# The first layer's beginning: half-tile loads, a fixed order of scaling and splitting, and more warming matmuls

## The chip, the cores and the metric

The kernel runs on one core of a Trainium2 chip. The metric is device time in microseconds of one execution, as the median of three runs. The engines are TensorE (PE, with its weight loads as PEld), VectorE (DVE), ScalarE (ACT), GpSimd (POOL) and SyncE (SP); SP issues nearly all DMAs here.

## What is computed

Two pre-norm decoder layers on 256 tokens of 1024 channels in float32. Each layer normalises, multiplies by one wide input projection, runs three groups of heads side by side, projects back, and then runs a squared-ReLU MLP:

```python
for l in range(DEPTH):                       # DEPTH = 2, x is (1, 256, 1024)
    h = rms_norm(x, ln1_gain[l])
    proj = h @ w_in[l]                       # 1024 x 2866, cut into 15 parts
    ...                                      # sparse attention, latent attention, retention
    x = x + mixed @ w_out[l]
    h = rms_norm(x, ln2_gain[l])
    x = x + jnp.square(jax.nn.relu(h @ w_up[l])) @ w_down[l]
return rms_norm(x, final_gain)
```

with `rms_norm(x, g) = x * rsqrt(mean(x*x) + eps) * g`. Only the beginning of layer 0 is touched by the change.

## The kernel before

**Products.** A float32 product is made of three float32r matmuls (`mm3`, L144 to L148): each operand is split into a high part, cast by ACT (L140), and a low part, source minus high part, by DVE (L141). x stands as 2 tiles t of 128 tokens, with 1024 channels in two halves h of 512; `xT` holds it transposed and split, 8 blocks of 128 channels, and is the stationary operand. The factor `rstd` of the norm is not in `xT`: it is applied when the accumulated result is taken out of PSUM by ACT (`scaled`, L570). The channel gain is in `xT`.

**The input projection** goes by chunks of columns in the order A, B2, B1, B3, rq, rk, rg, rv (`inproj`, L555). A chunk is loaded in units of 2 or 3 channel blocks; chunk A has 434 columns and four units of 2 blocks (434 KB each), so 48 matmuls: 12 per unit. Chunk A fills two accumulator banks, one per t, of the only two that the tag `acc` has; chunk B2 needs them next.

**The weight stream** (`Stream`, L265) hands out, in a fixed list, loads and splits of units. A raw unit lives in one of 5 raw buffers until it is split, its high and low part in one of 5 split buffers until its matmuls are done. Loads are issued by SP in order. Behind chunk A the list has small vectors, `uq` and `uk` (weights of the latent attention), B2, two sets of small tables (`w2s`, and `pos_t` in 16 DMAs of 8 KB, L404), `c1` (1056 KB of constants), B1, the four `w1` units (2 MB, L415), which are used straight from their raw buffers and not split, and B3.

**Order.** The framework orders each engine's instructions ahead of time, by priority and by the times that it reckons. `prio(key)` lifts a block by so many places (`split`: 800). `tc.issue_after(ins)` puts a block's instructions that are on the engine of `ins` behind it in that engine's queue.

**The beginning of layer 0.** SP issues c0 (identity and rope frequencies), half (0,0) of x, the gain g8, half (0,1), weight unit A0, all of tile 1 of x, then A1, A2, A3 (L167 to L179, L323). PE runs 8 warming matmuls of 128x128 (L176), then for each (t, h) in `norm_half` (L487) four transposes (L493); DVE multiplies 512 columns by the gain (L500), ACT casts them (L140), DVE subtracts (L141). Units A1 and A2 have their low part made by POOL (`START_POOL`). The sums of squares (`sum_sq`, L510, ACT) come behind the last half's cast, then `mean_sq` (DVE) and the power on POOL (L194) give `rstd`. The rope tables (L200) are some 30 small DVE instructions and two Sin on ACT (L228, L229); nothing ties their place.

Of the kernel before, what the change touches and what calls it, by code (L numbers as in the profile page):

```python
# [14 lines left out]
P = 128  # L15
# [28 lines left out]
    'pol': -100, 'norm': 100, 'act': 200, 'split': 800,  # L44
}

PIECES = {'A': 2, 'B1': 4, 'B2': 2, 'B3': 4, 'rk': 2, 'rg': 4, 'rv': 2, 'wo': 2, 'wu': 2}

START_POOL = (1, 2)

MAGIC = 12582912.0
PI_LO = 3.1415925
# [25 lines left out]
def tile_hybrid_trunk(  # L78
# [65 lines left out]
    def mm3(o, a, b, start, stop):  # L144

        nc.tensor.matmul(o, a[1], b[0], start=start, stop=False)  # L146
        nc.tensor.matmul(o, a[0], b[1], start=False, stop=False)  # L147
        nc.tensor.matmul(o, a[0], b[0], start=False, stop=stop)  # L148

    def bcast_row(t, row, n):  # L150
        nc.sync.dma_start(t, row.unsqueeze(0).broadcast_to([P, n]))
# [22 lines left out]
    ps_idle = acc("ps_idle")  # L174
    for _ in range(WARM):
        nc.tensor.matmul(ps_idle[:, 0:P], idle, idle, start=True, stop=True)  # L176
# [139 lines left out]
    def add_unit(key, pieces, n, eng=nc.vector):  # L316

        name = "_".join(str(z) for z in key)

        def load():  # L320
            raw = raw_tile(name)
            for view, src in pieces:
                nc.sync.dma_start(view(raw), src)  # L323
            return raw

        def split_(raw):
            p = hilo(name)
            m = n // PIECES.get('A0' if key[:2] == (0, 'A') else key[1], 1)
            for o in range(0, n, m):
                split(p[0][:, o:o + m], p[1][:, o:o + m], raw[:, o:o + m], eng)  # L330
            return p

        W.add(key, load, split_)
# [150 lines left out]
    xT2 = p1.tile([P, 8, 2, S], F32R, name="xT", tag="xT")  # L484
    xT = [xT2[:, :, i] for i in range(2)]

    def norm_half(t, h, gain, eng=nc.vector):  # L487
        sl = slice(h * 512, (h + 1) * 512)
        xg = scr("xg", [P, 512])
        ps = wk("ps_xT", "MN"[h])  # L490
        if gain is None:
            for j in range(4):
                nc.tensor.transpose(ps[:, j * P:(j + 1) * P], xs[:, t, h * 512 + j * P:h * 512 + (j + 1) * P], ident)  # L493
            if t == h == 0:

                ps_g = acc("ps_g")
                nc.tensor.transpose(ps_g[:, 0:8], g8, ident[0:8, 0:8])
                nc.vector.tensor_copy(gT, ps_g[:, 0:8])
            xg = xg.rearrange("p (k c) -> p k c", k=4)
            nc.vector.tensor_tensor(xg, ps.rearrange("p (k c) -> p k c", k=4),  # L500
                                    gT[:, 4 * h:4 * h + 4].unsqueeze(2).broadcast_to([P, 4, P]), op=ALU.mult)
            dst = (slice(None), slice(4 * h, 4 * h + 4), slice(t * P, (t + 1) * P))
            return split(xT[0][dst], xT[1][dst], xg)
# [24 lines left out]
    for l in range(DEPTH):  # L528
# [5 lines left out]
        rstd = p2.tile([P, 2], F32, name=L + "rstd", tag="rstd")  # L534
        hrstd = p2.tile([P, 2], F32, name=L + "hrstd", tag="hrstd")
        if l == 0:
            for t in range(2):
                for h in range(2):
                    last = norm_half(t, h, None)
            with tc.issue_after(last[0].ins):  # L540
                for t in range(2):
                    for h in range(2):
                        sum_sq(t, h, ss1)
        else:
            ss1 = ss_next
        for t in range(2):
            mean_sq(ms1, ss1, t)
            rsqrt(rstd[:, t:t + 1], ms1[:, t:t + 1])
            nc.gpsimd.tensor_scalar(hrstd[:, t:t + 1], rstd[:, t:t + 1], 0.5, None, op0=ALU.mult)

        if l == 0:
            rope_tables()
# [624 lines left out]
```

## Time and profile before

| | us |
|---|---|
| median of 3 runs (lowest, highest) | 675.86 (675.41, 676.44) |
| the profiled execution, its own time | 675.34 |
| its span, first to last instruction | 673.5 |
| PE busy in the span | 651.4 (97%) |
| DVE / ACT / POOL busy | 452.4 / 379.3 / 68.0 |

Times inside the trace count from the span's start. The profiled execution has 1.84 us around its span, and is 0.52 us below the median. A busy PE is a PE with an instruction in flight, at whichever clock; so a stretch with the lower granted clock counts as busy too.

### The profile page before, as it was taken

Reading aid. Unit: us, or ns where it says so; the run is one execution under the profiler, and the core shown is the slowest. Engines: PE = TensorE matmul, PEld = TensorE weight load, DVE = VectorE, ACT = ScalarE, POOL = GpSimd, SP = SyncE. Lnnn points to the kernel's source line nnn. Section 1 sums busy time; section 2 is a strip of 40 time slices with the busy share of each in tenths; the row PEclk is TensorE's granted clock in tenths of the full one; section 3 lists DMA queues with packets and bytes.
Section 4 is the critical chain, followed back from the end, with each engine's and each line's share of the span. In section 5 each row is a group of like instructions: output and inputs, shape, how many; then the busy total and the mean of one; then the engine's idle time right before and its main releaser. Section 6 shows DMA issues by size and latency. Waiting matters only on the chain.

```text
span 673.5 us, 10414 instructions
## 1 busy us (share of the span) xinstructions
PE 651.4 (97%) x3639; PEld 551.9 (82%) x3639; DVE 452.4 (67%) x1051; ACT 379.3 (56%) x887; POOL 68.0 (10%) x116
## 2 busy tenths in 40 slices
PE   7988999999999999999999999999999999999995
PEld 6987978676788888888889998876688888888884
DVE  6755967677756666666685597677686666666664
ACT  5857776364645454545466786637284454545442
POOL 3510401201000000000023132111100000000000
PEclk7999999999999999999999999999999999999999
DMA  7898544122865656565648574331275656565511
GB/s 232 261 186 257 168 126 123 44 94 68 269 204 165 218 169 215 167 215 167 175 139 200 168 240 133 93 95 34 92 254 181 220 169 208 172 203 181 195 62 62
DMA packets 79508, 111.58 MB, mean 166 GB/s; under 512 B 9432, under 2 KB 67680, under 8 KB 79328
## 3 DMA queue, kind: packets, MB, share of 16 engines
q1 hardware_dynamic: 79424, 110.92, 53.9%
q8 instruction: 28, 0.46, 0.3%
q14 instruction: 24, 0.20, 0.1%
q0 software_dynamic: 32, 0.00, 0.0%
HBM read 109.86 MB, written 1.05 MB: 165 GB/s over the span
## 4 chain that ended last, share of the span: by engine, by line
PE 87%; DMA 5%; DVE 4%; ACT 1%; issue 1%; SPq 1%; POOL 0%; POOLq 0%; ACTq 0%; DVEq 0%
PE ps_up L1023 17%; PE l_pd L146 9%; PE l_pd L147 9%; PE l_pd L148 8%; PE ps_up L1024 8%; PE l_po L146 2%; PE l_po L148 2%; PE l_po L147 2%; PE l_oT L856 2%; DMA raw_B<-in_w_in_dram 2%; PE l_B L146 1%; PE l_B L147 1%; PE l_B L148 1%; PE ps_pT L864 1%; PE ps_s L146 1%; DMA raw_wu<-in_w_up_dram 1%
## 5 line engine op out<-in xcount | busy, mean ns | idle before, releaser
L1023 PE MATMUL ps_up<-xT,hi_wu 128*128 128x512 f32 x512 | 180.0, 394 | 1.3 <-DVE u_s L1035 1.3
L1024 PE MATMUL ps_up<-xT,lo_wu 128*128 128x256 f32 x512 | 140.7, 279 | 0.0
L1023 PEld LDWEIGHTS ps_up<-xT,hi_wu 128*128 128x128 f32 x512 | 95.7, 187 | 24.0 <-DVE u_s L1035 1.7
L141 DVE TENSOR_TENSOR lo_wd<-raw_wd,hi_wd 128x1024 fp32r<-128x1024 f32 x64 | 78.2, 1225 | 52.5 <-ACT hi_wd L140 52.2
L147 PE MATMUL l_pd<-lo_wd,u_h 128*128 128x512 f32 x256 | 100.1, 391 | 0.0
L146 PE MATMUL l_pd<-hi_wd,u_l 128*128 128x512 f32 x256 | 100.1, 391 | 0.0
L148 PE MATMUL l_pd<-hi_wd,u_h 128*128 128x512 f32 x256 | 99.6, 389 | 0.0
L1024 PEld LDWEIGHTS ps_up<-xT,lo_wu 128*128 128x128 f32 x512 | 96.0, 188 | 1.7
L140 ACT CAST hi_wu<-raw_wu 128x512 fp32r<-128x512 f32 x128 | 72.5, 617 | 38.9 <-issue 28.1
L141 DVE TENSOR_TENSOR lo_wu<-raw_wu,hi_wu 128x512 fp32r<-128x512 f32 x128 | 82.2, 687 | 16.6 <-ACT hi_wu L140 16.4
L140 ACT CAST hi_wd<-raw_wd 128x1024 fp32r<-128x1024 f32 x64 | 67.0, 1049 | 32.1 <-PE l_pd L148 21.4
L146 PEld LDWEIGHTS l_pd<-hi_wd,u_l 128*128 128x128 f32 x256 | 48.0, 188 | 10.8
L148 PEld LDWEIGHTS l_pd<-hi_wd,u_h 128*128 128x128 f32 x256 | 48.1, 188 | 10.4
L147 PEld LDWEIGHTS l_pd<-lo_wd,u_h 128*128 128x128 f32 x256 | 48.1, 188 | 8.9
L140 ACT CAST u_h<-u_u 128x512 fp32r<-128x512 f32 x32 | 19.8, 620 | 55.4 <-DVE u_u L1037 55.4
L141 DVE TENSOR_TENSOR lo_B<-raw_B,hi_B 128x192 fp32r<-128x192 f32 (+1 forms) x80 | 28.7, 415 | 23.9 <-ACT hi_B L140 23.8
L1034 ACT COPY u_s<-ps_up 128x256 f32<-128x256 f32 x64 | 23.3, 368 | 36.1 <-PE ps_up L1024 36.1
L1035 DVE TENSOR_TENSOR u_s<-ps_up,u_s 128x256 f32<-128x256 f32 x64 | 26.7, 421 | 24.8 <-ACT u_s L1034 24.8
L140 ACT CAST hi_B<-raw_B 128x192 fp32r<-128x192 f32 (+1 forms) x80 | 25.1, 381 | 18.6 <-DMA raw_B<-in_w_in_dram 13.7
L146 PE MATMUL l_B<-hi_B,xT 128*128 128x384 f32 x96 | 32.9, 351 | 2.3 <-ACT q_sb L570 2.3
L141 DVE TENSOR_TENSOR u_l<-u_u,u_h 128x512 fp32r<-128x512 f32 x32 | 22.1, 691 | 17.8 <-ACT u_h L140 17.8
L148 PE MATMUL l_B<-hi_B,xT 128*128 128x384 f32 x96 | 32.4, 338 | 0.0
(321 smaller groups left out, 1246.5 us busy)
## 6 DMA issues: line engine op xcount, KB each, us to landing
raw_wu<-in_w_up_dram SPq DMA_DIRECT2D x64, 512.0 KB, 4.6
raw_wd<-in_w_down_dram SPq DMA_DIRECT2D x64, 512.0 KB, 4.2
raw_B<-in_w_in_dram SPq DMA_DIRECT2D x24, 384.0 KB, 3.6
raw_wo<-in_w_out_dram SPq DMA_DIRECT2D x10, 512.0 KB, 3.6
raw_A<-in_w_in_dram SPq DMA_DIRECT2D x8, 434.0 KB, 5.0
raw_wo<-in_w_out_dram SPq DMA_DIRECT2D x12, 256.0 KB, 3.8
raw_w<-in_cmp_w_k_dram SPq DMA_DIRECT2D x8, 256.0 KB, 6.3
raw_w<-in_cmp_w_v_dram SPq DMA_DIRECT2D x8, 256.0 KB, 5.8
```

Source lines behind the costliest of these rows:

```text
L140: a = nc.scalar.copy(out=hi, in_=src)
L141: b = eng.tensor_tensor(lo, src, hi.bitcast(F32), op=ALU.subtract)
L146: nc.tensor.matmul(o, a[1], b[0], start=start, stop=False)
L147: nc.tensor.matmul(o, a[0], b[1], start=False, stop=False)
L148: nc.tensor.matmul(o, a[0], b[0], start=False, stop=stop)
L856: nc.tensor.matmul(oT[gp, 0:384], kv_sb[kt][:, vi, gp], pTs[g][:, 0:384], start=i == 0, stop=False)
L864: last = nc.tensor.transpose(ps[:, r * P:(r + 1) * P], prs[g][:, r, o:o + P], ident)
L1023: nc.tensor.matmul(ps[j], w[0][:, o:o + P], x2, start=i == 0 and k == 0, stop=False)
L1024: nc.tensor.matmul(ps[j][:, 0:S], w[1][:, o:o + P], x2[:, 0:S], start=False, stop=i == 1 and k == 3)
L1034: nc.scalar.copy(sj, ps[j][:, S:512])
L1035: nc.vector.tensor_tensor(sj, ps[j][:, 0:S], sj, op=ALU.add)
```

## The change

Loads: c0 and g8 are issued by ACT instead of SP; SP issues half (0,0) of x, A0, half (1,0), A1, half (0,1), half (1,1), A2, A3. Scaling: instead of one multiplication of 512 columns, a cast and a subtraction, each block of 128 channels gets one ACT instruction straight from PSUM with the gain as scale, and one DVE instruction (gain times PSUM minus high part). Order: on ACT and DVE it is now half (0,0), A0, half (1,0), A1, half (0,1), half (1,1), A2, A3, and behind them the rope tables and the sums of squares; the transposes of the h = 1 halves stand behind unit A0's last matmul on PE. The units of A are split in two pieces instead of one, all on ACT and DVE. After the transposes of half (0,0) PE gets 6 more warming matmuls, after those of (1,0) 4 more.

```diff
-PIECES = {'A': 2, 'B1': 4, ...}
-START_POOL = (1, 2)
+PIECES = {'A0': 2, 'A': 2, 'B1': 4, ...}
+WARM_ON = (6, 4)
...
-    nc.sync.dma_start(c0s, c0)
+    nc.scalar.dma_start(c0s, c0)
+    nc.scalar.dma_start(g8, ln1_gain[0].rearrange("(k p) -> k p", p=P))
     nc.sync.dma_start(xs[:, 0, 0:512], xv[:, 0, 0:512])
-    nc.sync.dma_start(g8, ln1_gain[0].rearrange("(k p) -> k p", p=P))
-    nc.sync.dma_start(xs[:, 0, 512:D], xv[:, 0, 512:D])
...
     def late_start():
-        nc.sync.dma_start(xs[:, 1, :], xv[:, 1, :])
+        x_part(0, 1)
+        x_part(1, 1)
...
             add_chunk(l, "A", 1)
+            W.add("x0", lambda: x_part(1, 0))
+            add_chunk(l, "A", 2, 1)
             W.add("x1", late_start)
-            add_chunk(l, "A", 4, 1)
+            add_chunk(l, "A", 4, 2)
...
+    def norm_start(t, h, after=None, behind=None):
+        ps = wk("ps_xT", "MN"[h])
+        with tc.issue_after(behind.ins) if behind else nullcontext():
+            for j in range(4):
+                tr = nc.tensor.transpose(ps[:, j * P:(j + 1) * P], xs[:, t, ...], ident)
+        if t == h == 0:
+            ...                                   # g8 transposed, gT copied by DVE
+        if h == 0:
+            warm(WARM_ON[t], tr)
+        with (tc.issue_after(after[0].ins) if after else nullcontext()), \
+             (tc.issue_after(after[1].ins) if after else nullcontext()):
+            for j in range(4):
+                k, pj = 4 * h + j, ps[:, j * P:(j + 1) * P]
+                hi, lo = (z[:, k, t * P:(t + 1) * P] for z in xT)
+                a = nc.scalar.activation(hi, pj, AF.Copy, scale=gT[:, k:k + 1])
+                b = nc.vector.scalar_tensor_tensor(lo, in0=pj, scalar=gT[:, k:k + 1], in1=hi.bitcast(F32),
+                                                   op0=ALU.mult, op1=ALU.subtract)
+        return a, b
...
+            W.hold((l, "A", 2))
+            last = norm_start(0, 0)
+            last = split_next(1, last)
+            last = norm_start(1, 0, last)
+            at_start = [split_next(1, last)]
...
+        def start_rest(behind, ss1=ss1):
+            last = norm_start(0, 1, at_start[0], behind)
+            last = norm_start(1, 1, last, behind)
+            W.limit = None
+            last = split_next(2, last)
+            with tc.issue_after(last[0].ins), tc.issue_after(last[1].ins):
+                with prio("split"):
+                    rope_tables()
                 for t in range(2):
                     for h in range(2):
                         sum_sq(t, h, ss1)
...
             for i, ks in enumerate(KSETS[n]):
+                if i == 1 and (l, name) == (0, "A"):
+                    start_rest(last)
+                    factors()                     # mean_sq, rsqrt, half of rstd
```

`split_next(n, after)` splits the next n units of the stream behind `after` on ACT and DVE.

## Rows read from the trace of the kernel before

**Rows 1.** Busy time by stretch: stretch, each engine's busy us, granted clock, DMA share, GB/s.
```profile
0.00:23.50 23.50, 19.14 (x83) 16.93 (x84) 17.12 (x49) 15.77 (x30) 7.90 (x13) 0.85 0.76 219
23.50:47.10 23.60, 23.60 (x146) 23.08 (x144) 13.61 (x41) 15.57 (x46) 9.89 (x21) 1.00 1.07 265
47.10:67.10 20.00, 14.72 (x139) 13.35 (x137) 11.54 (x38) 14.04 (x39) 0.00 (x0) 1.00 0.68 214
67.10:673.50 606.40, 593.93 (x3276) 498.50 (x3276) 410.14 (x925) 333.92 (x776) 50.25 (x83) 1.00 0.51 158
```

**Rows 2.** PE's timeline: start, duration, engine, line, operation, [idle before it, releaser].
```profile
1.06 3.78 PE L176 MATMUL ps_idle<-idle 128*128 128x128 f32 x16 [1.06 <-DVE idle L173]
8.77 1.97 PE L493 MATMUL ps_xT<-c0s,xs 128*128 128x128 f32 x8 [1.83 <-DMA xs<-in_x_dram]
10.89 0.70 PE L146 MATMUL l_A<-hi_A,xT 128*128 128x434 f32 x1 [0.15 <-DVE xT L141]
...
16.22 0.47 PE L146 MATMUL l_A<-hi_A,xT 128*128 128x434 f32 x1 [0.65 <-DVE xT L141]
...
23.08 0.36 PE L148 MATMUL l_A<-hi_A,xT 128*128 128x434 f32 x1
```

**Rows 3.** Busy time by stretch, two stretches of 0.2 us around the clock's changes.
```profile
8.20:8.40 0.20, 0.00 (x0) 0.00 (x0) 0.20 (x2) 0.20 (x2) 0.00 (x0) 0.50 1.01 382
...
15.00:15.20 0.20, 0.20 (x2) 0.20 (x1) 0.20 (x1) 0.20 (x1) 0.20 (x1) 0.98 0.06 12
```

**Rows 4.** DVE's timeline in chunk A's stretch.
```profile
8.97 1.05 DVE L141 TENSOR_TENSOR lo_A<-raw_A,hi_A 128x868 fp32r<-128x868 f32 x1
...
11.43 2.10 DVE L141 TENSOR_TENSOR xT<-xg,xT 128x512 fp32r<-128x512 f32 x1
...
14.06 1.51 DVE L216 SCALAR_TENSOR_TENSOR rt<-rt 128x96 f32<-128x96 f32 x1
```

**Rows 5.** POOL's timeline in the first 20 us.
```profile
10.94 4.50 POOL L141 TENSOR_TENSOR lo_A<-raw_A,hi_A 128x868 fp32r<-128x868 f32 x2 [8.59 <-ACT hi_A L140]
18.24 0.99 POOL L194 TENSOR_TENSOR l_rstd<-l_ms,mhalf 128x1 f32<-128x1 f32 x1 [2.79 <-DVE l_ms L516]
```

**Rows 6.** Who waited for whom on PE, 0 to 110 us: total, times, longest.
```profile
PE l_B L146 <- ACT q_sb L570: 2.3, 1, 2.3
```

**Rows 7.** The chain that ended last, 36 to 68 us: start, duration, what.
```profile
41.16 6.90 DMA raw_B<-in_w_in_dram
...
67.09 0.41 PE l_rq L146
```

**Rows 8.** SP's timeline: start and duration of DMA issues.
```profile
15.18 0.38 SPq L323 DMA_DIRECT2D raw_B<-in_w_in_dram  x1
...
23.43 0.42 SPq L459 DMA_DIRECT2D c1s<-c_dram  x1
```

**Rows 9.** Groups by line and shape, 0 to 24 us: count, busy us, mean ns.
```profile
L500 DVE TENSOR_TENSOR xg<-ps_xT,gT 128x512 f32<-128x512 f32 x4 | 2.7, 681 | 0.0
L512 ACT ACTIVATE junk<-xs 128x512 f32<-128x512 f32 x4 | 2.5, 618 | 0.0
...
L389 DVE SCALAR_TENSOR_TENSOR lo_uq<-raw_uq,l_nrm,hi_uq 128x480 fp32r<-128x480 f32 x2 | 1.3, 705 | 0.0
L388 ACT ACTIVATE hi_uq<-raw_uq,l_nrm 128x480 fp32r<-128x480 f32 x2 | 1.3, 684 | 0.0
L388 ACT ACTIVATE hi_uk<-raw_uk,l_nrm 128x640 fp32r<-128x640 f32 x1 | 0.8, 817 | 0.0
```

**Rows 10.** ACT's timeline: first cast of A, a table load, a result taken out.
```profile
7.44 0.92 ACT L140 CAST hi_A<-raw_A 128x868 fp32r<-128x868 f32 x1 [5.42 <-DMA raw_A<-in_w_in_dram]
...
18.44 1.28 ACT L228 ACT_TABLE_LOAD   x1
19.74 0.28 ACT L228 ACTIVATE rt<-rt 128x96 f32<-128x96 f32 x1
...
21.63 0.61 ACT L570 ACTIVATE l_a<-l_A,l_rstd 128x434 f32<-128x434 f32 x1
```

More of the change, by code (lines that the diff above doesn't have):

```diff
@@ L147, in mm3 @@
         nc.tensor.matmul(o, a[0], b[1], start=False, stop=False)
-        nc.tensor.matmul(o, a[0], b[0], start=False, stop=stop)
+        return nc.tensor.matmul(o, a[0], b[0], start=False, stop=stop)
     def bcast_row(t, row, n):
@@ L166, in tile_hybrid_trunk, with warm, x_part @@
     g8 = p2.tile([8, P], F32, name="g8", tag="gain", bufs=1)
-    nc.sync.dma_start(c0s, c0)
+    nc.scalar.dma_start(c0s, c0)
+    nc.scalar.dma_start(g8, ln1_gain[0].rearrange("(k p) -> k p", p=P))
     nc.sync.dma_start(xs[:, 0, 0:512], xv[:, 0, 0:512])
-    nc.sync.dma_start(g8, ln1_gain[0].rearrange("(k p) -> k p", p=P))
-    nc.sync.dma_start(xs[:, 0, 512:D], xv[:, 0, 512:D])
     idle = scr("idle", [P, P])
     nc.vector.memset(idle, 0.0)
-    ps_idle = acc("ps_idle")
-    for _ in range(WARM):
-        nc.tensor.matmul(ps_idle[:, 0:P], idle, idle, start=True, stop=True)
+    ps_idle = att("ps_idle", "N")
+    def warm(n, behind=None):
+        with tc.issue_after(behind.ins) if behind else nullcontext():
+            for _ in range(n):
+                nc.tensor.matmul(ps_idle[:, 0:P], idle, idle, start=True, stop=True)
+    warm(WARM)
+    def x_part(t, h):
+        nc.sync.dma_start(xs[:, t, h * 512:(h + 1) * 512], xv[:, t, h * 512:(h + 1) * 512])
     def late_start():
-        nc.sync.dma_start(xs[:, 1, :], xv[:, 1, :])
+        x_part(0, 1)
+        x_part(1, 1)
     nc.gpsimd.dma_start(pos_i, positions.rearrange("o (t p) -> p (o t)", p=P))
@@ L329, in split_ @@
             for o in range(0, n, m):
-                split(p[0][:, o:o + m], p[1][:, o:o + m], raw[:, o:o + m], eng)
+                W.last = split(p[0][:, o:o + m], p[1][:, o:o + m], raw[:, o:o + m], eng)
             return p
@@ L352, in add_chunk @@
                                      wv[:, ks[0]:ks[-1] + 1, col:col + n])], m * n,
-                     nc.gpsimd if (l, name) == (0, "A") and i in START_POOL else nc.vector)
+                     nc.vector)
     def add_side(l, name, f):
@@ L485, in tile_hybrid_trunk @@
     xT = [xT2[:, :, i] for i in range(2)]
+    def norm_start(t, h, after=None, behind=None):
+        ps = wk("ps_xT", "MN"[h])
+        with tc.issue_after(behind.ins) if behind else nullcontext():
+            for j in range(4):
+                tr = nc.tensor.transpose(ps[:, j * P:(j + 1) * P], xs[:, t, h * 512 + j * P:h * 512 + (j + 1) * P],
+                                         ident)
+        if t == h == 0:
+            ps_g = acc("ps_g")
+            nc.tensor.transpose(ps_g[:, 0:8], g8, ident[0:8, 0:8])
+            nc.vector.tensor_copy(gT, ps_g[:, 0:8])
+        if h == 0:
[9 more added lines that the diff above has]
+        return a, b
     def norm_half(t, h, gain, eng=nc.vector):
@@ L490, in norm_half @@
         ps = wk("ps_xT", "MN"[h])
[L491 to L503, printed above, removed]
         eng.tensor_tensor(xg, xs[:, t, sl], gain[:, sl], op=ALU.mult)
@@ L508, in norm_half, with split_next @@
         return split(xT[0][dst], xT[1][dst], ps.rearrange("p (k c) -> p k c", k=4))
+    def split_next(n, after):
+        with tc.issue_after(after[0].ins), tc.issue_after(after[1].ins):
+            for _ in range(n):
+                while not W.units[W.done][1]:
+                    W.done += 1
+                W.split_to(W.done + 1)
+        return W.last
     def sum_sq(t, h, ss):
@@ L521, in split_mix @@
         split(mixT[0][dst], mixT[1][dst], src)
-    for u in W.units[:W.index["x1"] + 1]:
+    for u in W.units[:W.index[0, "A", 3] + 1]:
         u[2] = u[0]()
@@ L536, in tile_hybrid_trunk, with factors @@
         if l == 0:
-            for t in range(2):
-                for h in range(2):
-                    last = norm_half(t, h, None)
-            with tc.issue_after(last[0].ins):
+            W.hold((l, "A", 2))
[3 more added lines that the diff above has]
+            at_start = [split_next(1, last)]
+        else:
+            ss1 = ss_next
+        def factors():
+            for t in range(2):
+                mean_sq(ms1, ss1, t)
+                rsqrt(rstd[:, t:t + 1], ms1[:, t:t + 1])
+                nc.gpsimd.tensor_scalar(hrstd[:, t:t + 1], rstd[:, t:t + 1], 0.5, None, op0=ALU.mult)
+        def start_rest(behind, ss1=ss1):
[6 more added lines that the diff above has]
+                    rope_tables()
                 for t in range(2):
@@ L543, in tile_hybrid_trunk @@
                         sum_sq(t, h, ss1)
[L544 to L552, printed above, removed]
+        if l:
+            factors()
         mixT = [p1.tile([P, 8, S], F32R, name=f"{L}mixT{i}", tag=f"mixT{i}") for i in range(2)]
@@ L558, in inproj @@
             for i, ks in enumerate(KSETS[n]):
+                if i == 1 and (l, name) == (0, "A"):
+                    start_rest(last)
+                    factors()
                 w = W.get((l, name, i))
@@ L562, in inproj @@
                     for j, kt in enumerate(ks):
-                        mm3(ps[t][:, 0:n], (xT[0][:, kt, tk], xT[1][:, kt, tk]),
-                            [z[:, j * n:(j + 1) * n] for z in w], start=kt == 0, stop=kt == 7)
+                        last = mm3(ps[t][:, 0:n], (xT[0][:, kt, tk], xT[1][:, kt, tk]),
+                                   [z[:, j * n:(j + 1) * n] for z in w], start=kt == 0, stop=kt == 7)
             with prio(name):
```

2 lines of the change are left out of this document (1 added, 1 removed).

## The prediction, made before the change was run

> **What bounds the kernel now.** I read the busy time by stretches first [rows 1]. Behind 67.1 us PE is busy 594 of 606 us at full clock; nothing that the change touches lies there, and that part can only move as a whole. Three stretches lie ahead of it. From 23.5 to 47.1 us PE is never idle, and the DMA engines are full too (share 1.07). From 47.1 to 67.1 us PE is busy 14.7 of 20 us. From 0 to 23.5 us it counts as busy 19.1 us, but at a mean clock of 0.85.
>
> In the first stretch PE's timeline [rows 2] shows the losses. The warming matmuls end at 4.84 us. After the transposes of tile 0 PE waits 1.83 us, until 8.77, for the DMA of tile 1. The first product starts at 10.89. The granted clock falls to 0.50 at 8.2 us, in that wait, and is back at 15.0 us [rows 3]; a product takes 0.70 us in flight at 10.89 and 0.36 at 23.08 [rows 2]. The 48 products of chunk A run as 13 from 10.89 to 15.57 (0.36 each), then 0.65 us of waiting for DVE, then 35 from 16.22 to 23.44 (0.206 each). 48 x 0.206 = 9.9 us would do, and the stretch holds them for 12.55.
>
> DVE is why they start late. A subtraction of 512 columns, the size for which L500 takes 0.68 us [rows 9], took 2.10 us at 11.43, and a rope step of 96 columns took 1.51 us at 14.06 [rows 4]: both beside POOL's two subtractions of A1 and A2, 4.50 us from 10.94 [rows 5].
>
> The stretch behind 47.1 us was read from the chain and the waits. PE waits there 2.3 us for ACT's `q_sb` [rows 6], and ACT stands in order behind the cast of B3's first unit, whose DMA was issued at 41.16 and landed 6.90 us later [rows 7]. From that landing the chain goes DMA to split to DMA, and PE picks up at 67.09. So what counts for the end is when B3's load lands, not when PE gets there. A start that is 4 us earlier is worth 4 us only if the loads move 4 us too.
>
> **The change, part by part.** *Loads.* c0 and g8 leave SP's queue: one issue takes 0.4 us [rows 8], so half (0,0) starts some 0.45 us earlier, and A0 goes from fifth to second on SP. A0 landed at 7.44 [rows 10]; the bytes ahead of it fall from 604 KB to 344 KB, so I put it at 6.3 to 6.8, half (1,0) at 7.0 to 7.4, A1 at 8.3, A3 as before near 12 (the bytes are the same). Half (0,0) lands before the warming ends at 4.84, so its earlier issue gives nothing.
>
> *Scaling and splitting.* Removed on DVE: 4 gain multiplications of 0.68 us [rows 9] = 2.7 us; on POOL 4.5 us [rows 5], and with them the 2.10 - 0.68 = 1.4 and 1.51 - 0.25 = 1.3 us that DVE lost beside POOL (0.25 is my estimate for a lone step of 96 columns, from 0.68 for 512 with a fixed part). Added on DVE: A1 and A2, 2 x 1.05 us [rows 4]. The new small instructions aren't in the trace. An ACT one with a scale of 480 columns takes 0.684, of 640 takes 0.817 [rows 9]: 0.83 ns a column and 0.285 fixed, so 0.39 for 128 columns; without the fixed part it would be 0.14, and no more than 0.684. I take 0.36 and one each 0.27 us, since neighbours overlap by about 0.1 (two of 0.684 hold ACT for 1.27). For DVE 480 columns take 0.705 [rows 9]: between 0.19 (by share) and 0.705; I take 0.31, one each 0.24. Per half that is 1.2 us on ACT and 1.0 on DVE, against 0.6 and 1.36 before: ACT +2.3 us over four halves, DVE -1.4.
>
> *Order, forward from there.* gT is copied at about 5.9. Half (0,0): ACT 6.0 to 7.15, DVE to 7.5. A0 (halves of 434 columns, ACT about 0.5, DVE 0.6, from 0.92 and 1.05 for 868 [rows 10, 4]): high parts at 7.65 and 8.1, low at 8.25 and 8.8. Half (1,0): ACT to 9.2, DVE to 9.9. A1: ACT to 10.2, DVE to 11.1. PE starts products at 8.3 and ends unit A0 at 10.7; eight transposes, 0.9 us; unit A1 to 14.0. Halves (0,1) and (1,1): ACT to 13.4. A2: low part at 14.6 and 15.2; A3: 15.8 and 16.4. Unit A2 runs to 17.0, A3 to 19.4. So chunk A ends near 19.4 instead of 23.44: 4.0 us.
>
> *Warming.* 10 matmuls are 20 instructions (16 for 8 now [rows 2]), 0.11 us each at full clock and 0.236 at half: 2.2 to 4.7 us on PE, in the time in which it waited for tile 1 and for DVE. If data came sooner than I have it, they would cost up to 1 us at 8.3. What they are to buy: PE has no wait of 1.83 us, and I take it that the clock stays up.
>
> *New waits.* ACT: A0's casts wait for A0's landing, and all of (1,0) is queued behind them; the scaling of (0,1) waits for transposes that wait for unit A0 on PE, and A2, A3, the rope tables' Sin, the sums of squares and the casts of `uq` are behind it. The sums (4 of 0.62 = 2.5 us [rows 9]), the mean and POOL's power (0.99 us [rows 5]) must be done before chunk A can be taken out of its two banks, which B2 needs. They can't begin before 15.4 now: 15.4 + 2.5 + 0.3 + 1.0 = 19.2, just in time if they go first; each `uq` or `uk` cast that goes first puts 0.7 to 0.8 on top. The rope steps (16 ahead of Sin, at 0.24) share DVE with `uq` (1.4), `uk` (0.9) and B2's first unit (1.0): it is split by about 20 (the 1.4 from two of 0.705 [rows 9], the 0.9 and 1.0 from 640 and 768 columns at that rate). So B2 starts at 20 to 20.5 instead of 23.5: 3.0 to 3.5 us.
>
> *What is late next: the loads.* B2's first unit needs A1's raw buffer: issued at 15.18 before [rows 8], from 11.1 now. B2_1 and B2_2 need A2 and A3 (15.2 and 16.4). `c1`, at whose issue at 23.43 [rows 8] the full DMA stretch begins, stands behind B2_3 (needs `uq` split: about 18) and 16 `pos_t` issues of 0.4 us each. I put it at 20.4: 3.0 us. Between 1 us and 4.5 us is possible, since SP's order is worked out anew.
>
> **Sum.** 4.0 us at the end of chunk A, 3.0 to 3.5 at B2's start, 3.0 for the loads; the smallest counts. The profiled execution's 675.34 (a span of 673.5 and 1.84 around it) becomes 672.3; its place 0.52 below the median gives **672.9**. With the bounds (loads 1.5 to 4.5) the forecast's own range is 671.2 to 674.4.
>
> [...] The Sin load took 1.28 us at 18.44 and the Sin began at 19.74, 0.02 us behind it [rows 10]. [...]
>
> **Rivals.** *Swallowed.* The start comes earlier, but `c1` and `w1` don't: SP's small issues and `uq`'s buffer hold them where they are, B3's load lands at 47.5 to 48 as before, and PE only waits longer than 2.3 us. For it: DMA share 1.07 and SP in order; against it: the DMAs moved nothing near their rate from 15 to 23 us. Time: 675.4.
>
> *The clock falls all the same*, in a gap before (1,0) lands at 7 us, and stays down 6.8 us as before [rows 3]: 19 products instead of 33 in that time, 14 x 0.206 = 2.9 us lost. The end of A gains 1.1 to 1.5 us. Time: 674.5.
>
> *Late sums (slower).* The splits are lifted by 800 places and the sums by none. If `uq`, `uk`, two units of B2 (0.92 each) and Sin with its table go first on ACT, the sums begin at 15.4 + 1.3 + 0.8 + 1.8 + 1.75 = 21.05 (1.75 is the load of 1.28 [rows 10] and two Sin), and `rstd` is there at 21.05 + 2.5 + 0.3 + 1.0 = 24.9, the first bank free at 25.5 instead of 22.2 (21.63 + 0.61 [rows 10]). B2 starts at 25.6 instead of 23.5. It decides against the change from `rstd` later than 22.9. Time: 678.0.
>
> *More.* All loads move with PE and the order behind them stays tight: 671.0.
>
> **How the numbers follow.** Forecast 0.52, swallowed 0.18, clock 0.10, late sums 0.14, more 0.06. A measurement can tell about 0.2%, 1.35 us, from no change: the line lies at 674.5. Faster: forecast, more, and half of the clock's = 0.63; same: swallowed and the other half = 0.23; slower 0.14. The range goes from 670.6 (the bounds of the loads) to 677.4, which takes in the swallowed and clock cases and a mild form of the late sums.
>
> **What would show it.** Right: the first product at 8.3 to 8.8, granted clock 1.00 throughout, no DVE instruction of 512 columns above 0.8 us ahead of 16 us, chunk A's last product near 19.4, `c1` issued near 20.4, B3's load landing near 45. Wrong: a row with clock 0.50 behind 6 us; PE waiting on ACT's `l_a` at B2's start (late sums); `c1` at 23 us or a wait on `q_sb` far above 2.3 us (swallowed).

## The result, and the profile of the changed kernel

The changed kernel takes 684.72 us (median; 683.95 to 686.83) where the kernel before, beside it, took 675.63 (673.23 to 676.44): a ratio of 1.0141, interval 1.0118 to 1.0164. That is 9 us slower, where 672.9 was forecast. The profiled execution took 686.83 us with a span of 685.0, against 675.34 and 673.5 before. It is the slowest of its four, 2.1 us above their median, so the 11.5 us between the two profiled spans are some 2 us more than lies between the medians.

Busy time by stretch of the changed kernel (columns as in [rows 1]; the last row is cut so that it is as long as the last one of before):

```profile
0.00:23.50 23.50, 16.71 (x83) 14.76 (x84) 10.21 (x28) 11.39 (x27) 1.30 (x6) 0.92 0.69 205
23.50:47.10 23.60, 17.96 (x77) 17.02 (x77) 13.60 (x54) 14.99 (x44) 7.46 (x21) 0.79 0.61 196
47.10:67.10 20.00, 20.00 (x181) 19.33 (x180) 10.80 (x40) 14.27 (x38) 2.11 (x5) 1.00 0.63 143
67.10:78.60 11.50, 8.85 (x49) 8.23 (x48) 7.73 (x22) 9.22 (x22) 0.52 (x1) 0.97 0.88 276
78.60:685.00 606.40, 594.84 (x3276) 499.44 (x3274) 410.18 (x925) 333.54 (x774) 50.27 (x83) 1.00 0.51 158
```

The last 606.40 us hold 3276 matmuls in both kernels, 594.84 us busy against 593.93 [rows 1]. So all of the 11.5 us lies ahead of them. In the stretch from 23.5 to 47.1, where PE had been busy without a gap at clock 1.00 and the DMA engines at 1.07, PE is now busy 17.96 us at 0.79 and the DMA engines at 0.61.

PE's timeline says where the time was lost (columns as in [rows 2]):

```profile
7.27 0.23 PE L506 MATMUL ps_g<-c0s,g 8*128 8x8 f32 x1
...
10.95 0.46 PE L146 MATMUL l_A<-hi_A,xT 128*128 128x434 f32 x1 [1.98 <-ACT hi_A L140]
...
21.26 1.09 PE L146 MATMUL l_A<-hi_A,xT 128*128 128x434 f32 x2 [3.57 <-ACT hi_A L140]
...
28.36 0.36 PE L148 MATMUL l_A<-hi_A,xT 128*128 128x434 f32 x1
34.37 0.90 PE L645 MATMUL ps_cT<-c0s,l_a 128*128 128x128 f32 x3 [5.64 <-ACT l_a L616]
```

Two waits stand out. One of 3.57 us lies inside chunk A, which ends at 28.72 instead of 23.44; one of 5.64 us lies between chunk A and B2. The clock falls in each. It is 0.50 in both of these stretches (same view as above), and 15 products of chunk A and 16 of B2 run at 0.36 and 0.32 us each instead of 0.20 and 0.175:

```profile
24.00:26.00 2.00, 2.00 (x7) 1.85 (x6) 2.00 (x7) 2.00 (x6) 0.00 (x0) 0.50 0.77 259
35.00:39.00 4.00, 4.00 (x15) 4.00 (x14) 1.79 (x13) 3.53 (x14) 1.97 (x4) 0.50 0.66 192
```

The cause of the first wait is in the timelines of ACT and DVE. Each instruction of the new pair waits for the other engine's:

```profile
7.73 0.37 ACT L515 ACTIVATE xT<-ps_xT,gT 128x128 fp32r<-128x128 f32 x1 [4.65 <-DVE gT L507]
8.52 0.37 ACT L515 ACTIVATE xT<-ps_xT,gT 128x128 fp32r<-128x128 f32 x1 [0.42 <-DVE xT L516]
```
```profile
7.53 0.17 DVE L507 COPY gT<-ps_g 128x8 f32<-128x8 f32 x1 [6.53 <-PE ps_g L506]
8.13 0.35 DVE L516 SCALAR_TENSOR_TENSOR xT<-ps_xT,gT,xT 128x128 fp32r<-128x128 f32 x1 [0.44 <-ACT xT L515]
```

ACT's starts are 0.79 us apart: ACT 0.37, DVE 0.35, and the handing over. Nothing overlaps within a half. DVE's waiting for ACT is by data (it reads the high part). ACT's waiting for DVE is not: the next block's ACT instruction needs nothing that DVE makes. For 16 blocks it comes to 12.6 us on both engines.

The cause of the second wait is in SP's and ACT's timelines:

```profile
18.72 0.39 SPq L331 DMA_DIRECT2D raw_B<-in_w_in_dram  x1
...
20.59 0.42 SPq L469 DMA_DIRECT2D c1s<-c_dram  x1
21.06 0.43 SPq L151 DMA_DIRECT2D l_gng<-in_ret_gn_gain_dram  x1
21.59 0.38 SPq L151 DMA_DIRECT2D gain_b<-in_ln_gain_dram  x1
...
23.36 12.01 SPq L331 DMA_DIRECT2D raw_B<-in_w_in_dram  x7
43.24 2.81 SPq L423 DMA_DIRECT2D raw_w<-in_cmp_w_k_dram  x4
```
```profile
31.83 1.97 ACT L140 CAST hi_B<-raw_B 128x384 fp32r<-128x384 f32 x4 [4.08 <-DMA raw_B<-in_w_in_dram]
33.70 1.13 ACT L616 ACTIVATE l_a<-l_A,l_rstd 128x434 f32<-128x434 f32 x2
```

In the kernel before, B2's second and third unit were issued at 17.33 and `c1` at 23.43 [rows 8 has the latter]. Now `c1`, `gng` and `gain_b`, some 1.7 MB, go ahead of these two units, which land at 31.8 to 32.8. ACT has their casts in its queue ahead of taking chunk A out of its banks (L616), so it stands idle for 4.08 us, the last 3.1 of them with chunk A finished and `rstd`, which the taking out needs, ready at 28.7 on POOL. The chain of work that ended last has the same steps: the load from 23.91 to 32.78, two casts, `l_a` at 33.80, PE at 34.37.

From there everything is 11 to 12.4 us later: `w1` is issued at 43.24 (30.81 before), B3's first unit at 53.54 (41.16), and `l_rq` starts at 78.00 (67.09 [rows 7]).

### The profile page after: what moved, and what is told of

Same layout as the page of the kernel before. It is cut to its first block, busy times and chain, and to the rows that moved or that the text cites. A ratio compares the mean times of both kernels' runs of the same rounds, so it can differ in the third digit from the quotient of the medians.

```text
span 685.0 us, 10473 instructions
## 1 busy us (share of the span) xinstructions
PE 658.4 (96%) x3659; PEld 558.8 (82%) x3659; DVE 452.5 (66%) x1065; ACT 383.4 (56%) x903; POOL 61.7 (9%) x114
## 3 DMA queue, kind: packets, MB, share of 16 engines
HBM read 109.86 MB, written 1.05 MB: 162 GB/s over the span
## 4 chain that ended last, share of the span: by engine, by line
PE 91%; DVE 3%; DMA 2%; ACT 2%; issue 1%; POOL 0%; POOLq 0%; ACTq 0%; DVEq 0%
PE ps_up L1069 17%; PE ps_up L1070 9%; PE l_pd L146 8%; PE l_pd L147 8%; PE l_pd L148 8%; PE l_po L146 2%; PE l_po L148 2%; PE l_B L146 2%; PE l_B L148 2%; PE l_B L147 2%; PE l_po L147 2%; PE l_oT L902 2%; PE ps_pT L910 1%; DMA raw_B<-in_w_in_dram 1%; PE ps_s L146 1%; DMA raw_rq<-in_w_in_dram 1%
## 5 line engine op out<-in xcount | busy, mean ns | idle before, releaser
L146 PE MATMUL l_B<-hi_B,xT 128*128 128x384 f32 x96 | 34.0, 363 | 0.0
L148 PE MATMUL l_B<-hi_B,xT 128*128 128x384 f32 x96 | 33.3, 347 | 0.0
```

Of the source, the lines that this page charges most:

```text
L148: return nc.tensor.matmul(o, a[0], b[0], start=False, stop=stop)
```

## The experiments

All compare with the kernel before on the same chip, where it took 675.3 to 675.8. "A" gives chunk A's first product and its end, "B2" B2's first product, then come the issues of `c1`, of B2's second unit, of `w1` and of B3's first unit, and `l_rq`'s first product, all from the profiled execution, in us. That is one execution for each row, and it can lie up to 3 us from the median beside it (e4 3.0, e13 2.3 and the changed kernel 2.1 us above; e10 and e14 2.3 below).

| kernel | median | ratio (interval) | A | B2 | c1 | B2's 2nd | w1 | B3 | l_rq |
|---|---|---|---|---|---|---|---|---|---|
| before | 675.63 | 1 | 10.89–23.44 | 23.5 | 23.43 | 17.33 | 30.81 | 41.16 | 67.09 |
| changed | 684.72 | 1.0141 (1.0118–1.0164) | 10.95–28.72 | 34.92 | 20.59 | 23.36 | 43.24 | 53.54 | 78.00 |
| e1_acts_first | 678.03 | 1.0038 (1.0013–1.0063) | 8.37–21.24 | 22.70 | 21.86 | 22.38 | 34.79 | 45.80 | 69.72 |
| e2_four_banks | 678.65 | 1.0043 (1.0023–1.0062) | 9.76–23.31 | 25.62 | 20.50 | 21.02 | 36.52 | 48.66 | 71.70 |
| e3_wide | 682.85 | 1.0102 (1.0084–1.0120) | 9.12–23.23 | 32.67 | 20.50 | 24.11 | 39.52 | 50.00 | 75.1 |
| e6_c1_late | 680.96 | 1.0062 (1.0039–1.0084) | 11.26–29.17 | 31.01 | 25.97 | 23.23 | 37.29 | 47.14 | 71.46 |
| e4_no_warm_on | 683.12 | 1.0092 (1.0067–1.0118) | 8.60–27.13 | 32.30 | 20.79 | 23.47 | 39.32 | 50.33 | 75.00 |
| e9_b2_first | 678.22 | 1.0039 (1.0014–1.0064) | 8.43–21.29 | 24.32 | 24.76 | 17.66 | 31.72 | 42.73 | 68.99 |
| e10_b2_gain_first | 676.78 | 1.0021 (1.0004–1.0038) | 8.42–20.60 | 23.13 | 24.57 | 17.44 | 30.50 | 41.69 | 68.20 |
| e11_b2_first_no_warm | 676.62 | 1.0024 (1.0007–1.0041) | 7.34–21.55 | 23.83 | 23.64 | 17.93 | 30.80 | 41.40 | 67.64 |
| e14_c1_early | 676.52 | 1.0007 (0.9994–1.0020) | 9.16–21.02 | 22.48 | 14.88 | 17.82 | 29.30 | 42.00 | 67.05 |
| e15_c1_early_no_warm | 677.94 | 1.0028 (1.0009–1.0046) | 7.80–22.77 | 24.25 | 14.78 | 19.16 | 30.55 | 42.81 | 68.5 |
| e13_before_c1_early | 676.84 | 1.0029 (1.0013–1.0046) | 10.79–23.59 | 23.67 | 15.65 | 17.49 | 30.73 | 41.27 | 71.2 |
| e8_no_pool | 675.47 | 0.9989 (0.9969–1.0009) | 10.91–22.39 | 22.47 | 24.95 | 17.59 | 31.84 | 42.30 | 67.83 |

The kernels e1 to e6 undo one part of the change each; e9 to e11, e14 and e15 undo or move several, to see what is left; e13 and e8 alter the kernel before.

**1. The order inside a half.** The same instructions, four of ACT written ahead of four of DVE.

```diff
             for j in range(4):
                 k, pj = 4 * h + j, ps[:, j * P:(j + 1) * P]
+                a = nc.scalar.activation(xT[0][:, k, t * P:(t + 1) * P], pj, AF.Copy, scale=gT[:, k:k + 1])
+            for j in range(4):
+                k, pj = 4 * h + j, ps[:, j * P:(j + 1) * P]
                 hi, lo = (z[:, k, t * P:(t + 1) * P] for z in xT)
-                a = nc.scalar.activation(hi, pj, AF.Copy, scale=gT[:, k:k + 1])
                 b = nc.vector.scalar_tensor_tensor(lo, in0=pj, ...)
```

> The changed kernel, with one thing moved: in each half tile the four ACT instructions (L515) are written ahead of the four DVE ones (L516) instead of in pairs. In the changed kernel each ACT instruction of a half waits for the DVE instruction before it, 0.79 us a block, 16 blocks = 12.6 us. Ping-pong theory: without that wait ACT spends about 0.28 us a block, the sixteen blocks end some 6 us earlier, chunk A's last product comes at 20 to 22 us instead of 28.4, and the time falls from 684.7 to between 672 and 677. Loads theory (what costs is that c1 and the gains are issued ahead of B2's second unit): 682 to 684, since the order of the loads isn't touched. Clock theory (what costs is the half clock by itself): the stretches at 0.50 stay, 682 to 685.

Measured: 678.03, 6.7 us less than the changed kernel, and 1 us above the range that the first theory gave. ACT's and DVE's timelines:

```profile
6.70 1.14 ACT L514 ACTIVATE xT<-ps_xT,gT 128x128 fp32r<-128x128 f32 x4 [3.61 <-DVE gT L507]
7.71 1.02 ACT L140 CAST hi_A<-raw_A 128x434 fp32r<-128x434 f32 x2
...
21.69 1.39 ACT L618 ACTIVATE l_a<-l_A,l_rstd 128x434 f32<-128x434 f32 x2
```
```profile
7.87 1.13 DVE L518 SCALAR_TENSOR_TENSOR xT<-ps_xT,gT,xT 128x128 fp32r<-128x128 f32 x4 [1.21 <-ACT xT L514]
```

Four now take 1.14 us on ACT and 1.13 on DVE, and ACT is at the next unit's casts while DVE works. Chunk A ends at 21.24, 7.5 us earlier. But SP's order was still `c1` (21.86) ahead of B2's second unit (22.38). ACT takes chunk A out ahead of that unit's cast here, so B2 begins at 22.70 and PE waits inside it, the clock falls to 0.50 (products 0.32 apart), and `l_rq` is 2.6 us later than before:

```profile
28.59 1.01 PE L146 MATMUL l_B<-hi_B,xT 128*128 128x384 f32 x2 [3.22 <-ACT hi_B L140]
```

**2. What ties ACT to DVE.** The pairs stay as they are written, but each block of a half has a PSUM bank that differs from its neighbour's.

```diff
-        ps = wk("ps_xT", "MN"[h])
+        pss = [wk("ps_xT", "MN"[j % 2]) for j in range(4)]
...
-                tr = nc.tensor.transpose(ps[:, j * P:(j + 1) * P], ...)
+                tr = nc.tensor.transpose(pss[j][:, 0:P], ...)
```

> The changed kernel, pairs kept as they are, but each 128-channel block of a half is transposed into a PSUM bank of its own (four banks a half instead of one). If the wait of ACT for DVE comes from their sharing one bank, it goes, and the time comes within 2 us of the run with the four ACT instructions first (672 to 677; the second half's transposes may wait a little for banks). If it comes from both writing parts of the same tile xT, nothing changes: 684 to 686, blocks 0.79 us apart.

```profile
8.12 1.14 ACT L515 ACTIVATE xT<-ps_xT,gT 128x128 fp32r<-128x128 f32 x4 [5.04 <-DVE gT L507]
```
```profile
8.52 1.13 DVE L516 SCALAR_TENSOR_TENSOR xT<-ps_xT,gT,xT 128x128 fp32r<-128x128 f32 x4 [0.43 <-ACT xT L515]
```

ACT's four run in 1.14 us without a wait, although each pair is still written ACT, DVE, ACT, DVE. DVE starts 0.40 us behind ACT and keeps pace. So the tie was the shared bank: two engines that read one bank were put in turn by the kernel's waits, whichever columns they read. (Each of the four blocks has a PSUM tile of its own here too, so no run tells the bank from the tile.) It isn't `xT`, which both write here too. 678.65, 6 us less than the changed kernel and within 2 us of e1, as expected for the bank, though above the 677 given with it. Chunk A ends 2 us later than in e1, since `gT` comes 1.4 us later here (7.92 against 6.50; the same 12 warming instructions ahead of it took 2.24 us against 1.50) and transposes wait for banks (1.0 us, on DVE).

**3. The scaling put back alone.** One gain multiplication of 512 columns, one cast and one subtraction for each half, in the new order.

```diff
-            for j in range(4):
-                a = nc.scalar.activation(hi, pj, AF.Copy, scale=gT[:, k:k + 1])
-                b = nc.vector.scalar_tensor_tensor(lo, in0=pj, ...)
+            ...                              # xg: 512 columns
+            nc.vector.tensor_tensor(xg, ps..., gT[:, 4 * h:4 * h + 4]..., op=ALU.mult)
+            ...                              # dst: where they go in xT
+            a, b = split(xT[0][dst], xT[1][dst], xg)
```

> The changed kernel with the scaling alone put back: one gain multiplication of 512 columns on DVE, one cast, one subtraction for each half, in the new order; nothing alternates between ACT and DVE block by block. Theory that the paired blocks cost some 1.9 us a half: chunk A ends 4 to 6 us earlier than in the changed kernel (22 to 24 against 28.7), 677 to 680. Rival, that the new order and the loads cost it whatever the scaling is: 683 to 685.

Each expectation came true in one half. Chunk A ends at 23.23, as the first had it (and as early as before the change), and the time is 682.85, next to the second's 683 to 685:

```profile
32.11 0.90 PE L644 MATMUL ps_cT<-c0s,l_a 128*128 128x128 f32 x3 [8.88 <-ACT l_a L615]
```
```profile
20.50 0.42 SPq L469 DMA_DIRECT2D c1s<-c_dram  x1
20.96 1.18 SPq L151 DMA_DIRECT2D l_gng<-in_ret_gn_gain_dram  x1
22.24 0.78 SPq L151 DMA_DIRECT2D gain_b<-in_ln_gain_dram  x1
24.11 10.12 SPq L331 DMA_DIRECT2D raw_B<-in_w_in_dram  x7
```
```profile
30.61 0.92 ACT L140 CAST hi_B<-raw_B 128x384 fp32r<-128x384 f32 x2 [6.30 <-DMA raw_B<-in_w_in_dram]
```

PE waits 8.88 us at the same place as in the changed kernel. Chunk A is as early as before, and 7 us are lost all the same. Two things meet: on SP `c1` and the gains go ahead of B2's second unit, and on ACT that unit's cast stands ahead of `l_a`. The load order alone does not cost so much. In e1 and e2 `c1` goes ahead of that unit too (the gains do not), but ACT empties at least one of chunk A's two banks ahead of its cast (`l_a` at 21.69 and 24.64), and 2.8 and 3.4 us are lost. No run has e3's load order with `l_a` in front. Taking out the alternation gives back only 1.9 us here, as these two lie behind it.

**4. The load order put back alone.** `c1`, `gng` and `gain_b` behind B2's last unit on SP; the alternation stays.

```diff
-            W.add("c1", lambda: nc.sync.dma_start(c1s, c1) and None)
+            def c1_load():
+                with tc.issue_after(W.dma[0, "B2", 3].ins):
+                    nc.sync.dma_start(c1s, c1)
+            W.add("c1", c1_load)             # gng and gain_b likewise
```

> The changed kernel with the issues of c1 (1056 KB), the retention gain (160 KB) and the ln2 gain (512 KB) put behind B2's last load on SP; they stood ahead of B2's second unit. Loads theory: B2's second unit has 1.7 MB less in front of it, 4.4 us at the 390 GB/s of that stretch, lands at about 27.5 instead of 31.8, chunk A is taken out at 29 to 30 instead of 34, and the time falls by 3 to 5 us, to 680 to 682. Ping-pong theory: it is a consequence that costs on top, so the same fall is possible, but the split chain still ends at 23 us and chunk A at 28.4.

680.96, 3.8 us less than the changed kernel. The wait for `l_a` falls from 5.64 to 1.54 us, and no clock dip follows it (1.00 from 30 to 35 us); the 3.57 us inside chunk A stay, and it ends at 29.17. So in the changed kernel the load order costs about 4 us and the alternation about 6 us (e1, e2). These are not fixed prices that add up: with four ACT first, putting the load order back changes the median by 0.2 us (e9 against e1, below).

**5. The added warming matmuls left out.** `WARM_ON = (0, 0)`.

> The changed kernel without the ten added warming matmuls. Ping-pong theory: the gain vector's transpose no longer stands behind six warming matmuls, the first scaling starts at about 6 instead of 7.7 us, so up to 1.5 us sooner unless the clock falls earlier; 683 to 686. Clock theory: the warming is what holds the clock up to 19 us; without it the clock falls at about 9 us, chunk A's first 24 products run at 0.36 instead of 0.20, and the time goes up by 2 to 4 us to 687 to 689.

683.12: 1.6 us less, not more; the two intervals in the table touch, so this is at the edge of what can be told apart. Without them `gT` is there earlier and the first product starts at 8.60 instead of 10.95, at a clock of 0.57 in the mean from 10 to 15 us. In the changed kernel the 12 instructions of the first six stand on PE ahead of the transpose of `g8` (7.27, in PE's timeline above), and ACT waits for `gT` with all the rest behind it.

**6. Both put back at once.** Four ACT ahead of four DVE, and on SP `w2s` and `pos_t` of the second set, `c1`, `gng` and `gain_b` behind B2's third unit. e10 adds the transpose of `g8` ahead of the added warming; e11 has no added warming.

```diff
+                with tc.issue_after(W.dma[l, "B2", 2].ins) if z and l == 0 else nullcontext():
                     nc.sync.dma_start(w2s[:, z], w2[l])
                     ...                      # pos_t; c1, gng and gain_b likewise
...
+            tr = nc.tensor.transpose(ps_g[:, 0:8], g8, ident[0:8, 0:8])     # e10: warm() goes behind this
```

> The changed kernel with the four ACT instructions first, and on SP, behind B2's third load: the second half of the small tables (w2s and eight pos_t), c1 and the two gains. With ACT first alone B2's second unit was issued at 22.4 us, behind the eight pos_t and c1, though its raw buffer was free at about 18; PE waited 3.2 us for it and then ran 16 products at half clock. Order-of-loads theory: it is issued at about 18, lands at 22 to 23, that wait and the half clock go, 3 to 5 us less than 678.0: 673 to 675, not slower than the kernel before (675.3). Rival (full DMA engines: whatever goes first, c1 and w1 land no earlier, and the wait reappears at B3): 676 to 678.

> As the one before, and the gain vector's transpose stands ahead of the six warming matmuls on PE instead of behind them. In the changed kernel gT was copied at 7.5 us, with ACT first alone at 6.5. It comes at 5.2 to 5.9 then. If the first scaling bounds the start, everything of chunk A up to the DMA of unit A3 moves by 0.6 to 1.2 us and the time by 0 to 1 us: 672.5 to 675. If the loads bound it, nothing changes.

> ACT first and B2 first as two runs above, without the ten added warming matmuls. Clock theory: the clock falls at about 8 to 9 us in the wait for half (1,0) and stays at 0.50 for some 6 us, during which 17 products run at 0.36 instead of 0.20: 2 to 3 us more than with the warming, 675 to 678. If the warming is worth nothing (the changed kernel without it was not slower): within 1 us of the run with it.

678.22, 676.78 and 676.62: the loss is gone but for 1 to 3 us, and there is no gain; e9 and e10 miss their ranges. Chunk A ends at 20.6 to 21.6, 2 to 3 us earlier than before; but B2 starts at 23.13 to 24.32 (23.5 before), `w1` is issued at 30.50 to 31.72 (30.81 before), B3's first unit at 41.40 to 42.73 (41.16), and `l_rq` starts at 67.64 to 68.99 (67.09). The earlier end is gone at B2's start already, since PE waits 2.72, 1.97 and 1.97 us for `l_a`. Two rows of e9, ACT's and PE's:

```profile
22.51 0.92 ACT L140 CAST hi_B<-raw_B 128x384 fp32r<-128x384 f32 x2 [0.65 <-DMA raw_B<-in_w_in_dram]
```
```profile
24.01 0.55 PE L654 MATMUL ps_cT<-c0s,l_a 128*128 128x128 f32 x3 [2.72 <-ACT l_a L625]
```

The cast of B2's second unit still stands ahead of `l_a` (23.34 in e9), in e10 and e11 without a wait for its landing. So of the changed kernel's two faults the second is made smaller here, not taken out. Behind this wait the clock falls again in e9 and e10, not in e11 (1.00 from 15 to 30 us): it is 0.55 from 24.3 to 28.0 us and 0.51 from 23.1 to 26.0.

**7. Does it help to clear the way for the loads?** The DMA engines have room ahead of 23 us (a share of 0.44 from 14 to 16 us before). `c1` is issued right behind B2's first unit, some 8 to 10 us earlier: in e13 in the kernel before, in e14 on top of e10, in e15 on top of e11.

```diff
-        add_chunk(l, "B2")
+        add_chunk(l, "B2", 1)
+        if l == 0:
+            def c1_load():
+                with tc.issue_after(W.dma[0, "B2", 0].ins):
+                    nc.sync.dma_start(c1s, c1)
+            W.add("c1", c1_load)
+        add_chunk(l, "B2", None, 1)
```

> The kernel before, with one load moved: c1 (1056 KB) is issued right behind B2's first unit, near 15.6 us instead of 23.43, into a stretch in which the DMA engines are busy at 0.44 to 0.80. Theory that the DMAs behind B2's start set l_rq and not chunk A's end: 1056 KB leave the full stretch (4.2 us at 250 GB/s), B3's load is issued 2 to 4 us earlier than 41.16, l_rq's first product comes near 64 to 65 instead of 67.1, 672 to 674 us. Rival: the raw buffers, which come free only as PE and the splits go on, hold B1, w1 and B3 where they are: 675 to 676. Second rival: c1 now stands in the way of B2's second to fourth unit, PE waits for hi_B at 25 us: 677 or more.

> The changed kernel with the four ACT instructions ahead of the four DVE ones, the gain's transpose ahead of the added warming, and the small loads behind B2's third unit; new is that c1 is issued right behind B2's first unit (near 15 us instead of 24.6). Theory that the loads swallow the earlier end of chunk A: with c1 out of the full stretch both gains add up, chunk A ends at 20 to 21, B2 starts near 23, B3's load is issued at 37 to 39 instead of 41.7, 671 to 673. Rival, buffers: 676 to 677 as without the move. Rival, c1 ahead of B2's units: PE waits 2 us or more near 27 us, 678 or more.

> As the last kernel (four ACT ahead of four DVE, c1 right behind B2's first unit, small loads behind the third), but with no added warming matmuls at all, so that the gain's transpose has none ahead of it either. Theory that the added warming buys nothing on the path, since the clock's dip costs less than the matmuls' own time and chunk A's end is not what counts: first product 7.4 instead of 9.16, clock partly 0.50 between 8 and 12 us, chunk A ends within 0.7 us of 20.9, 675 to 676.5. Rival, that warming is needed: chunk A ends at 22.5 or later, 677.5 or more. A version that beats the kernel before would have to come in under 674.1; I give that 0.15.

e13: 676.84, the rival and a little worse. With 1056 KB out of the full stretch, `w1` and B3's first unit are issued at 30.73 and 41.27, where they were. So the bytes of `c1` ahead of them did not hold them. The three largest of SP's waits from 25 to 66 us in e13 (releaser: total, times, longest) are for landings and for DVE's low parts, with which a raw buffer comes free:

```profile
SPq L324 <- DMA raw_B<-in_w_in_dram: 5.6, 3, 3.0
SPq L416 <- DVE lo_B L141: 5.5, 4, 2.1
SPq L324 <- DVE lo_B L141: 5.3, 4, 1.6
```

For B3 the rate of the loads is not cleared. From 31 to 41 us the DMA engines are full in e13 too (a share of 1.09, 1.14 before), and the chain that ended last comes to B3's issue through a unit of B1 that was issued at 29.74 and took 8.39 us to land:

```profile
29.74 8.39 DMA raw_B<-in_w_in_dram
```

Its `l_rq` at 71.2, 4 us later than before, is that of an execution 2.3 us above the median.

e14 comes out level with the kernel before, 1.0007 (0.9994 to 1.0020). Its loads do move: `w1` to 29.30, and the first unit of `rq` to 54.22 from 55.72. But `l_rq` starts at 67.05, as before (67.09). ACT's timeline in e14:

```profile
60.63 0.99 ACT L140 CAST hi_rq<-raw_rq 128x960 fp32r<-128x960 f32 x1 [0.24 <-DMA raw_rq<-in_w_in_dram]
61.65 1.28 ACT L719 ACT_TABLE_LOAD   x1
62.94 0.51 ACT L719 ACTIVATE pm<-pm,mla_m 128x256 f32<-128x256 f32 x1
...
65.45 1.08 ACT L140 CAST hi_rk<-raw_rk 128x480 fp32r<-128x480 f32 x2
66.43 0.57 ACT L626 ACTIVATE l_kv<-l_B,l_rstd 128x384 f32<-128x384 f32 x1
```

Before, ACT waited 1.34 us at 65.47 for `rk`'s DMA, and `l_kv` came at 66.46. Now `rk` is there in time, but a table load of 1.28 us, which the kernel before doesn't have between 57 and 68 us, has come into the queue ahead, and `l_kv` starts at 66.43. The change itself brings it. Before, Sin ran at 19.74 [rows 10], and the load for the next Exp came with `l_gate`; with the rope tables moved back, `l_gate` runs ahead of Sin, and the load for the next Exp falls to `pm`. First the kernel before, then e14, where L237 is Sin:

```profile
25.64 1.28 ACT L592 ACT_TABLE_LOAD   x1
26.93 0.22 ACT L592 ACTIVATE l_gate<-l_gate 128x18 f32<-128x18 f32 x1
```
```profile
26.43 0.22 ACT L648 ACTIVATE l_gate<-l_gate 128x18 f32<-128x18 f32 x1
...
28.29 1.28 ACT L237 ACT_TABLE_LOAD   x1
```

The changed kernel has this load at 72.59, and every version of it in the table has it but e2, where an `l_gate` still runs behind Sin; the kernel before, e8 and e13 do not have it. What it costs is not measured, as no run puts Sin back; its 1.28 us are about as much as e10 and e11 lose.

e15, the same as e14 without the added warming, is 1.4 us slower than e14; its chunk A ends 1.75 us later, at 22.77. Expected were 675 to 676.5; 677.94 and the end of chunk A are what its rival had. So the medians speak for leaving the added warming out by 1.6 us in the changed kernel (e4) and in e9 (against e11), where `gT` is behind it, by 0.2 in e10 (against e11), where `gT` is ahead, and against it by 1.4 in e14. As the intervals of all four pairs touch or overlap, no value can be given for it. No kernel beat the one before.

**8. POOL's part in the kernel before.** `START_POOL = ()`: A1 and A2 are split by DVE.

> The kernel before with one part of the change: units A1 and A2 split by DVE instead of POOL. The prediction had DVE lose 2.7 us beside POOL's two subtractions and pay 2.1 us for doing them: the DVE instructions of 2.10 and 1.51 us fall to about 0.7 and 0.25, chunk A ends 0 to 1 us earlier, 674 to 676. If DVE is the bound there and nothing is slowed by POOL: DVE's last instruction of chunk A comes 2 us later, 676 to 678.

675.47, a ratio of 0.9989 (0.9969 to 1.0009): no difference. Chunk A ends 1.05 us earlier (22.39), as DVE no longer loses time beside POOL (its four subtractions of 512 columns take 0.68 us each in the mean; before they took 1.04, one of them 2.10 [rows 4]), but `c1` (24.95) and B3's first unit (42.30) are issued later, and `l_rq` starts at 67.83.

## Why the prediction was wrong, point by point

**Cost of the pairs: the first step that failed.** The forecast took 0.27 us for each ACT and 0.24 for each DVE instruction, "since neighbours overlap", 1.2 and 1.0 us for each half. The sizes were about right: 1.14 and 1.13 for four in e1. What failed is that they overlap as written. In the changed kernel a half takes 0.79 x 4 = 3.2 us on both engines, since the blocks of a half share a PSUM bank (e2). The prediction put A2's low part at 15.2; the trace starts it at 21.23.

**Load order: the second step that failed.** "`c1` ... stands behind B2_3": the forecast took the list's order for SP's, though it also said that SP's order is worked out anew. `c1` was issued at 20.59, as forecast (20.4). But it went ahead of B2's second unit. What was counted as a gain of 3.0 us was the loss: the large load came early because it overtook the loads that PE needed first, and with it behind them 3.8 us come back (e6).

**Late sums: right place, half of the reason.** PE does wait for `l_a`, as the rival said. But the sums were done at 27.7 and `rstd` at 28.7, with chunk A ending at 28.72, and with the load order put back (e6) the wait is 1.54. What held ACT was the cast of a unit not landed, standing in order ahead of `l_a`. That casts of B2 would go first was in the rival, priced at 678.0; that one of them would wait there for its landing was not. Both failures together make it 684.7.

**`gT` at 5.9: failed, small.** It came at 7.53, behind the added warming. The forecast charged that warming "up to 1 us at 8.3" and did not see that the transpose of `g8` is behind it. e4 puts that at 1.6 us, at the edge of the noise. In e10, with that order mended, `gT` comes at 5.83. The first product is within the forecast's 8.3 to 8.8 there (8.42) and in e1 (8.37, with `gT` at 6.50).

**Chunk A's end at 19.4:** 20.6 at best (e10). The gain from the order and from DVE freed of POOL is there, 2.8 us instead of 4.0.

**The clock.** It held 1.00 up to 19 us, as taken, with PE idle for 1.98 us in between. It fell to 0.50 in the two new waits, of 3.57 and 5.64 us, which the forecast didn't have. The forecast's 0.236 us for a warming instruction "at half" is 3.78 us over 16 of them [rows 2], and the trace has the granted clock at 1.00 there (1.06 to 4.84). The added ones took 0.15 and 0.13 us each in the changed kernel (12 in 1.85, 8 in 1.06), at 1.00.

**Loads 3.0 us earlier.** Wrong even with four ACT first and the load order put back. The times of e9 to e14, 676.5 to 678.2, are near the swallowed rival's 675.4 (chance 0.18), but they do not come about in its way. It had PE reach B2 earlier and wait longer for `q_sb`. In e9 to e11 PE reaches B2 no more than 0.4 us earlier, because of `l_a`, and it waits 1.45 and 1.69 us for `q_sb` in e10 and e11, less than the 2.3 before. In e14 B2 starts 1.0 us earlier and `w1` is issued 1.5 us earlier, and a table load stands at the end. Of what the rival named, SP's issues, a buffer and full DMA engines, e13 decides only that the bytes of `c1` were not it.

**A term put at nothing: the place of Sin.** The forecast weighed Sin's table load ahead of the sums. It did not see that with Sin behind `l_gate` the next Exp's load of 1.28 us moves from `l_gate` to `pm`, into ACT's queue ahead of `l_kv`.

**Sums.** Three small numbers do not come out of the prediction's own rows: 675.86 less 4.5 is 671.4 and not 671.2; the 670.6 of the range has no working; and 128 columns at 0.83 ns are 0.11 us and not 0.14. The miss does not hang on them.

Open is which buffer or load holds `w1` in e10 and B3 in e10 and e14 at their old times, and why e13 comes out 1.4 us slower than the kernel before. Versions in which the casts of B2 stand behind `l_a` on ACT, or Sin ahead of `l_gate`, were not tried.

## What to carry to other kernels

When a wide instruction is cut into blocks on two engines, look at which buffers the engines share, not only at the data that passes between them: four blocks in one PSUM bank ran in turn here, at the sum of both durations and the handing over (0.79 us for 0.37 and 0.35), and writing all of one engine's blocks first gave 6 us back. When an edit shifts readiness times under a planner, read the order that each in-order queue gets out of it before adding up gains: here one large early load and one cast ahead of a result cost more than the whole edit could give. And an earlier start is worth only what the last queue lets through: ask for each following load what frees its buffer, and for each activation function that is moved who has to load a table behind it (1.28 us here).

## What the runs showed of the hardware that was not expected

In this kernel ACT and DVE reading different columns of one PSUM bank did not overlap, 0.79 us for a pair; in different banks four pairs took 1.5 us from ACT's first start to DVE's end (8.12 to 9.65), 0.38 each. The traces show waits between the instructions and can't tell whether the chip would also have stalled. Taken in turn, a pair cost 0.37 + 0.35 us and 0.07 for the handing over.

A load of an activation table took 1.28 us in e14 at 61.65, with the instruction before it ending 0.03 us ahead and the next 0.01 us behind. Moving one function moved the load to another function 36 us later (25.64 before, 61.65 in e14).
